# Six rounds of an output projection instead of four, and the small softmax-weight operations on GpSimd at ordinary priority

## The chip, the cores and the metric

The kernel runs on one core of a Trainium2 chip. The metric is the device time of one execution in microseconds; less is better. The engines are named as the profile names them: PE (matrix multiply; PEld is its weight load), DVE (vector), ACT (scalar and activation functions), POOL (GpSimd) and SP (issues the DMAs). Each engine works through its own instruction list in order.

## The reference, cut to what matters

One layer of an encoder, 1024 rows of 1024 columns, all in float32:

```
hn  = rms_norm(x);  q,k,v,glu,qm = split(hn @ w_in)
# A: 8 heads of 64, three dilated windows, merged by softmax weights of their denominators
attn = sum_p softmax_p(lse_p) * attention_p(rotary(norm(q)), rotary(norm(k)), v)
# B: gated unit, depthwise convolution over 31 rows, layer norm, silu
c    = silu(layer_norm(conv31(ga * sigmoid(gg))))
# C: 4 heads of 64 into 256 memory tokens
mo   = softmax(norm(qm) @ km.T / 8) @ vm
h    = x + concat(attn, c, mo) @ w_out          # 1024 -> 1024: eight blocks of 128 inputs
out  = h + (silu(fg) * fu) @ w_down,  fg,fu = split(conv3(rms_norm(h) @ w_up))   # 2816 wide
```

## The kernel before, in words

**Stages.** By time of the profiled execution: the input projection with the convolution and heads 0 to 5 beside it (to about 445 us), then heads 6 and 7 and the four memory heads, with the output projection reaching to 613 us, then the feed-forward part up to the end (1327.6 us).

**How the order is written.** Work is written as Python generators, advanced one step each tick (`Steps.tick`). Their order of emission, shifted by an offset from `PRIOS` (a larger number means that the instructions are wanted earlier), gives each instruction a priority; a scheduler with a model of times then fixes, before the run, each engine's list. At run time an instruction whose input is late holds up all behind it on its engine.

**The output projection** (`out_projections`, L1087). The concat of the three groups is eight blocks k of 128 inputs: k = 0 to 3 are the pairs of attention heads, 4 and 5 the convolution, 6 and 7 the pairs of memory heads. Each block and each half of its weights is split into a high and a low part, and a product takes three matmuls (high by high, high by low, low by high). `ROUNDS` lists which blocks are summed in one go: a round waits until its blocks are there, goes over the eight row tiles and two column halves (16 PSUM tiles, 3 matmuls of 512 columns per block in each, L1098), and `add_out` (L1110, DVE) adds each PSUM tile onto the residual `x_sb`. Two PSUM tiles (`proj`) are in use at a time. The last round also starts, row tile by row tile, the norm of the feed-forward part (L1163), and once its blocks are written the memory of the attention stage is released.

**Where blocks and weights wait.** The blocks of the last round lie in the tiles `mx_last`, the others in `mx` or `mx_more`, two blocks in each; `room_for` picks. The weights of `w_out` are loaded in the order of `ROUNDS` (L600 to L605), four blocks resident at a time (8 `w_hi`, 8 `w_lo`), and a block's weights are freed when its round is done.

**Softmax weights** (`softmax_weights`, L295), once per head, after its scores: the negated maxima and the denominators of the dilated pattern go through DRAM (8 stores, 4 loads, SP) to come into row order (`stat`); nine small DVE operations of 8 columns (L314 to L325) and one Exp on ACT (L318) make two weights per row; PE turns them (L329), DVE copies them (L332), SP stores them (L335, L336). `weigh` (L455) loads them spread over the head's columns (L467), multiplies and adds on POOL (L479, L484; DVE for the last half of pair 3), and ACT and DVE split the result into the block's parts (L291, L293). `head` also reloads q, k (L345 to L348) and v (L392, L393) on SP, converts q on POOL (L352 to L355), evacuates transposed probabilities on ACT and DVE (L272, L273) and adds halves of its output on POOL (L418).

Of the kernel before, what the change touches and what calls it, by code (L numbers as in the profile page):

```python
# [12 lines left out]
AF = mybir.ActivationFunctionType  # L13
OP = mybir.AluOpType
# [21 lines left out]

EARLY = 12

PRIOS = {"softmax_weights": 1000, "weigh": 500, "memory_values": -60, "memory_heads": 60, "add_out": 200}

ROUNDS = [[0], [4, 5], [1, 6, 7], [2, 3]]


def constants():
# [28 lines left out]
class Steps:  # L73
# [47 lines left out]
    def tick(self):  # L121
# [4 lines left out]
        for w in self.work[:]:  # L126
            with self.tc.high_priority(offset=PRIOS.get(w.__name__, 0)):
                if next(w, self) is self:
# [4 lines left out]
def block(tc, a, out):  # L133
    nc = tc.nc
    pe, act, dve, pool, sp = nc.tensor, nc.scalar, nc.vector, nc.gpsimd, nc.sync
# [23 lines left out]
    expo = cpool.tile([128, 4], F, name="expo")  # L159
# [20 lines left out]
    def count(key):  # L180
        stored[key] = stored.get(key, 0) + 1
# [23 lines left out]
    def room_for(k):  # L205


        if not keeping:
            return "mx_part"
        if k in ROUNDS[-1]:  # L210
            return "mx_last"
        before = [j for ks in ROUNDS[: round_of[k]] for j in ks if j not in kind_of]
        for name in keeping:
# [3 lines left out]

    round_of = {k: n for n, ks in enumerate(ROUNDS) for k in ks}

# [75 lines left out]
    def softmax_weights(h, stat, stat2):  # L295


        for k in range(8):
            sp.dma_start(st_d[h][k].rearrange("(r s) c n -> s r (c n)", r=4),
                         stat2[16 * k : 16 * k + 16].rearrange("s r c n -> s r (c n)"))  # L300
        yield
        there = stat[:, 1].rearrange("p u c n -> p u (c n)")
        sp.dma_start(there[0:64], st_d[h][1:8:2].rearrange("k p c n -> p k (c n)"))
        sp.dma_start(there[64:128, 0:3], st_d[h][2:7:2].rearrange("k p c n -> p k (c n)"))
        for c in range(2):
            sp.dma_start(stat[64:128, 1, 3, c], st_d[h][0, :, 1 - c])
        st.free("stat2")
        for _ in range(4):
            yield
        w = yield from st.new("w", [128, 2, 2, 4])  # L310
        wd = yield from st.new("wd", [128, 4, 2, 4])
        nm, d = (stat[:, :, :, :, i].rearrange("p g u c -> p g c u") for i in range(2))
        one = wd[:, 2]
        dve.tensor_tensor(one, nm[:, 0], nm[:, 1], OP.min)  # L314
        for g in range(2):
            dve.tensor_tensor(w[:, g], one, nm[:, g], OP.subtract)
        yield
        act.activation(w, w, AF.Exp)  # L318
        yield
        for g in range(2):  # L320
            dve.tensor_tensor(wd[:, g], w[:, g], d[:, g], OP.mult)
        dve.tensor_tensor(one, wd[:, 0], wd[:, 1], OP.add)
        dve.reciprocal(wd[:, 3], one)
        for g in range(2):
            dve.tensor_tensor(w[:, g], w[:, g], wd[:, 3], OP.mult)  # L325
        st.free("stat", "wd")
        yield
        ps = yield from st.new("z", [128, 512])
        pe.transpose(ps[0:16, 0:128], w.rearrange("p g c u -> p (g c u)"), ident)  # L329
        yield  # L330
        rows = yield from st.new("rows", [16, 128])
        dve.tensor_copy(rows, ps[0:16, 0:128])  # L332
        st.free("z", "w", "rows")
        for g in range(2):
            sp.dma_start(w_d[h][0, g, 64 : S + 64].rearrange("(u p) -> u p", p=128), rows[8 * g : 8 * g + 8])  # L335
            sp.dma_start(w_d[h][:, g, 0:64], rows[8 * g + 7 : 8 * g + 8, 64:128])  # L336
        count(("w", h))

    def head(h):
# [44 lines left out]
        else:  # L384
            st.kept["qk"] = 0
        st.start(softmax_weights(h, stat, stat2))
        while stored.get(("v", h // 4), 0) < NT:
            yield
# [171 lines left out]
    with tc.tile_pool(name="p1", bufs=1, side="right") as p1:  # L560
# [20 lines left out]
        def load_chunks(chunks):  # L581
            for c in chunks:
                w = 256 // c.n
                for k2 in range(KT // 2):
# [13 lines left out]
                    yield  # L598
            for k in sum(ROUNDS, []):
                for half in range(2):  # L600
# [486 lines left out]
        def out_projections():  # L1087
            for ks in ROUNDS:
                if ks is ROUNDS[-1]:
                    count("last round")  # L1090
                for k in ks:
                    while k not in mixed or (k, 1) not in wo:
                        yield
                for t in range(NT):
                    for half in range(2):
                        ps = yield from st.new("proj", [128, 512])
                        for n, (k, i, j) in enumerate(passes(ks)):
                            pe.matmul(ps, mixed[k][i][:, 128 * t : 128 * t + 128], wo[k, half][j],  # L1098
                                      start=(n == 0), stop=(n == 3 * len(ks) - 1))
                            if n % 6 == 5 and n < 3 * len(ks) - 1:  # L1100
                                yield
                        st.start(add_out(ps, x_sb[t][:, 512 * half : 512 * half + 512]))
                        yield
                    if ks is ROUNDS[-1]:
                        st.start(ffn["norm"](t))
                for k in ks:
                    st.free("w_hi", "w_lo", "w_hi", "w_lo", kind_of[k], kind_of[k])
# [258 lines left out]
```

## Time and profile before

| | us |
|---|---|
| median of 3 runs (lowest, highest) | 1325.08 (1323.47, 1330.56) |
| the profiled execution's own time | 1329.41 |
| its span on the core | 1327.6 |

Busy over the span: PE 1202.5 us (91%), DVE 857.2 us (65%), POOL 745.5 us (56%), ACT 629.1 us (47%). Times below are counted from the start of the span. A row of the timeline gives start, length, engine, line, operation and, in brackets, how long the engine had been idle before it and what it then waited for; a row of a group gives busy time and the mean ns of one instruction.

### The profile page before, as it was taken

How to read it: one execution, taken by the hardware profiler on the slowest of the kernel's cores; microseconds unless marked ns; L12 is line 12 of the kernel's file. 1: busy time of each engine (PE TensorE's matmuls, PEld its weight loads, DVE VectorE, ACT ScalarE, POOL GpSimd, SP SyncE). 2: the span in 40 equal slices, each digit the busy share in tenths (PEclk: the TensorE clock that was granted, in tenths of full speed). 3: DMA queues.
4: the chain of work that ended last, by engine and by line, in shares of the span. 5: the costliest groups of instructions: out<-in, count | busy, mean ns of one | idle time of the engine just before them, and what ended most of it. 6: DMA issues, size and time to landing. Idle time of an engine off the chain costs nothing. (4 is left out here: it accounts for less than half of the span.)

```text
span 1327.6 us, 18490 instructions
## 1 busy us (share of the span) xinstructions
PE 1202.5 (91%) x6287; PEld 1015.5 (76%) x6287; DVE 857.2 (65%) x1312; ACT 629.1 (47%) x1288; POOL 745.5 (56%) x721
## 2 busy tenths in 40 slices
PE   4899888799988587888798999999999999999997
PEld 4888887799967565676586888888888888888886
DVE  6748779786776555648668878888888652224222
ACT  5663165467865576425344444444444443333331
POOL 4834284595772443236557666666766645555552
PEclk8999988899979888899699999999999999999999
DMA  7363425565485641043122222222222254447443
GB/s 257 103 175 104 146 78 165 161 200 152 118 286 157 163 121 42 8 142 113 31 64 79 80 80 87 87 67 86 87 79 72 80 176 149 149 145 249 163 144 119
DMA packets 166554, 164.80 MB, mean 124 GB/s; under 512 B 20322, under 2 KB 125756, under 8 KB 166460
## 3 DMA queue, kind: packets, MB, share of 16 engines
q1 hardware_dynamic: 166460, 163.63, 40.0%
q8 instruction: 49, 0.80, 0.3%
q14 instruction: 45, 0.37, 0.1%
HBM read 121.51 MB, written 42.08 MB: 123 GB/s over the span
## 5 line engine op out<-in xcount | busy, mean ns | idle before, releaser
L916 PE MATMUL proj<-w_hi,hnT 128*128 128x256 f32 x896 | 191.7, 301 | 24.7 <-ACT raw L831 10.9
L1207 POOL TENSOR_TENSOR up_lo<-dn_raw,up_hi 128x512 fp32r<-128x512 f32 x88 | 131.5, 1516 | 118.4 <-ACT up_hi L1206 107.4
L916 PEld LDWEIGHTS proj<-w_hi,hnT 128*128 128x128 f32 x896 | 153.5, 203 | 28.3 <-ACT raw L831 11.7
L1207 POOL TENSOR_TENSOR up_lo<-up_sum,up_hi 128x512 fp32r<-128x512 f32 x88 | 153.2, 1751 | 26.8 <-ACT up_hi L1206 23.4
L1207 POOL TENSOR_TENSOR up_lo<-up_raw,up_hi 128x512 fp32r<-128x512 f32 x66 | 100.8, 1529 | 102.3 <-ACT up_hi L1206 94.7
L1207 DVE TENSOR_TENSOR up_lo<-dn_raw,up_hi 128x512 fp32r<-128x512 f32 x44 | 57.4, 1305 | 151.7 <-ACT up_hi L1206 144.1
L1206 ACT ACTIVATE up_hi<-dn_raw 128x512 fp32r<-128x512 f32 x132 | 75.2, 624 | 164.7 <-issue 115.0
L1333 PE MATMUL ps_dn<-up_lo,up_hi 128*128 128x512 f32 x352 | 137.0, 390 | 0.1
L1333 PE MATMUL ps_dn<-up_hi,up_lo 128*128 128x512 f32 x352 | 136.5, 389 | 0.0
L1333 PE MATMUL ps_dn<-up_hi 128*128 128x512 f32 x352 | 134.9, 389 | 0.0
L916 PE MATMUL proj<-w_lo,hnT 128*128 128x256 f32 x448 | 133.8, 299 | 0.6 <-POOL w_lo L623 0.6
L635 POOL TENSOR_TENSOR w_lo<-w_raw,w_hi 128x512 fp32r<-128x512 f32 x44 | 64.9, 1484 | 95.3 <-ACT w_hi L633 91.4
L1225 PE MATMUL ps_a<-A,up_hi 128*128 128x512 f32 x352 | 113.9, 395 | 0.0
L1225 PE MATMUL ps_c<-S,up_hi 128*128 128x512 f32 x352 | 110.7, 395 | 0.0
L418 POOL TENSOR_TENSOR u<-u,other 64x512 f32<-64x512 f32 (+2 forms) x40 | 44.5, 1121 | 88.6 <-ACT u L414 87.4
L916 PEld LDWEIGHTS proj<-w_lo,hnT 128*128 128x128 f32 x448 | 90.9, 203 | 1.2 <-POOL w_lo L623 1.2
L979 DVE SCALAR_TENSOR_TENSOR conv<-conv,cwT 128x1009 f32<-128x1009 f32 (+14 forms) x60 | 88.2, 1470 | 0.6
L1206 ACT ACTIVATE up_hi<-up_sum 128x512 fp32r<-128x512 f32 x88 | 54.6, 624 | 58.3 <-PE ps_c L1225 45.3
L278 PE MATMUL turn<-identr,prob 128*128 128x128 f32 x320 | 61.4, 299 | 21.3 <-DVE pt L273 14.6
L1225 PEld LDWEIGHTS ps_c<-S,up_hi 128*128 128x128 f32 x352 | 65.9, 187 | 16.1
L1225 PEld LDWEIGHTS ps_a<-A,up_hi 128*128 128x128 f32 x352 | 65.9, 187 | 16.0
L1333 PEld LDWEIGHTS ps_dn<-up_lo,up_hi 128*128 128x128 f32 x352 | 66.1, 188 | 14.5 <-POOL up_lo L1207 1.0
(234 smaller groups left out, 3127.1 us busy)
## 6 DMA issues: line engine op xcount, KB each, us to landing
up_raw<-w_up SPq DMA_DIRECT2D x92, 256.0 KB
dn_raw<-w_down SPq DMA_DIRECT2D x88, 256.0 KB
g_d<-yg SPq DMA_DIRECT2D x22, 512.0 KB
dn_raw<-g_d SPq DMA_DIRECT2D x44, 256.0 KB
x<-x SPq DMA_DIRECT2D x16, 512.0 KB
qk_d<-out SPq DMA_DIRECT2D x32, 256.0 KB
qk<-qk_d SPq DMA_DIRECT2D x16, 512.0 KB
w_raw<-w_in SPq DMA_DIRECT2D x40, 128.0 KB
```

What stands on the lines that cost most here:

```text
L278: pe.transpose(ps[:, i], blocks[g + i], ident)
L418: pool.tensor_tensor(o, o, m, OP.add)
L635: (dve if next(chunk_no) < EARLY else pool).tensor_tensor(lo, raw, f32(hi), OP.subtract)
L916: pe.matmul(ps[:, :256], lhs[i][:, k], c.parts[k][j], start=(k == 0 and i == 0 and j == 0), stop=(k == KT - 1 and i == 1))
L979: dve.scalar_tensor_tensor(acc[:, c0:c1], conv_in[i][:, c0 + k - 15 : c1 + k - 15], w, acc[:, c0:c1], OP.mult, OP.add)
L1206: act.activation(hi, src, AF.Copy)
L1207: adder.tensor_tensor(lo, src, f32(hi), OP.subtract)
L1225: pe.matmul(ps, w[i][:, k], ops[x][j][:, k], start=(first and n == 0), stop=(n == 3 * KH - 1), skip_group_check=not first)
L1333: pe.matmul(ps, gk[i][:, 128 * t : 128 * t + 128], wk[half][j], start=(k == 0 and m == 0), stop=(k == NF - 1 and m == 2))
```

## The change

The rounds are cut and put in another order; the weights of `w_out` and the places of the blocks follow from the same list (blocks 3 and 7, not 2 and 3, are now those of the last round). The raised priorities of `softmax_weights` and `weigh` are gone. The nine DVE operations of a head become nine POOL operations, in another form: the difference of the two maxima (twice, one for each sign), Relu and then Exp with scale -1 on ACT, and the reciprocal as the square of a power of -0.5 (`expo` holds -0.5).

```diff
-PRIOS = {"softmax_weights": 1000, "weigh": 500, "memory_values": -60, "memory_heads": 60, "add_out": 200}
+PRIOS = {"memory_values": -60, "memory_heads": 60, "add_out": 200}
-ROUNDS = [[0], [4, 5], [1, 6, 7], [2, 3]]
+ROUNDS = [[0], [4, 5], [1], [2], [6], [3, 7]]
@@ softmax_weights
-        dve.tensor_tensor(one, nm[:, 0], nm[:, 1], OP.min)
         for g in range(2):
-            dve.tensor_tensor(w[:, g], one, nm[:, g], OP.subtract)
+            pool.tensor_tensor(w[:, g], nm[:, g], nm[:, 1 - g], OP.subtract)
         yield
-        act.activation(w, w, AF.Exp)
+        act.activation(w, w, AF.Relu)
+        act.activation(w, w, AF.Exp, scale=-1.0)
         yield
         for g in range(2):
-            dve.tensor_tensor(wd[:, g], w[:, g], d[:, g], OP.mult)
-        dve.tensor_tensor(one, wd[:, 0], wd[:, 1], OP.add)
-        dve.reciprocal(wd[:, 3], one)
+            pool.tensor_tensor(wd[:, g], w[:, g], d[:, g], OP.mult)
+        pool.tensor_tensor(one, wd[:, 0], wd[:, 1], OP.add)
+        pool.tensor_tensor(wd[:, 3], one, expo[:, 0:1, None].to_broadcast([128, 2, 4]), OP.pow)
+        pool.tensor_tensor(wd[:, 3], wd[:, 3], wd[:, 3], OP.mult)
         for g in range(2):
-            dve.tensor_tensor(w[:, g], w[:, g], wd[:, 3], OP.mult)
+            pool.tensor_tensor(w[:, g], w[:, g], wd[:, 3], OP.mult)
```

## Rows read from the trace of the kernel before

**Rows 1.** Windows: from:to and length, busy time of each engine, PE clock, DMA.

```profile
449.00:461.00 12.00, 0.00 (x0) 0.00 (x0) 4.57 (x17) 5.38 (x16) 4.79 (x5) 0.61 0.38 91
449.00:545.00 96.00, 61.56 (x321) 48.30 (x321) 54.82 (x176) 64.17 (x171) 40.02 (x54) 0.80 0.30 83
545.00:578.00 33.00, 32.89 (x140) 26.28 (x139) 14.50 (x21) 4.66 (x7) 2.08 (x2) 0.97 0.00 0
760.00:800.00 40.00, 40.00 (x173) 32.14 (x172) 33.11 (x28) 18.01 (x27) 27.49 (x18) 1.00 0.27 90
```

**Rows 2.** Windows of the output projection's matmuls (L1098) alone: PE, PEld, clock, DMA.

```profile
449.00:545.00 96.00, 1.98 (x7) 1.16 (x7) 0.80 0.30 83
545.00:578.00 33.00, 31.48 (x130) 24.72 (x131) 0.97 0.00 0
```

**Rows 3.** Timeline of PE around the wait of round [1, 6, 7].

```profile
447.51 0.39 PE L1098 MATMUL proj<-w_hi,mx_more 128*128 128x512 f32 x1
...
461.60 1.94 PE L278 MATMUL turn<-identr,prob 128*128 128x128 f32 x8 [12.75 <-DVE pt L273]
...
464.67 2.26 PE L287 MATMUL o<-pt,v 128*128 128x256 f32 x9 [1.13 <-DMA v<-vr_d]
...
578.45 0.39 PE L1098 MATMUL proj<-w_hi,mx_last 128*128 128x512 f32 x1
```

**Rows 4.** Timeline of DVE: last step of blocks 2, 6 (both halves), 3 and 7.

```profile
462.66 1.10 DVE L293 TENSOR_TENSOR mx_last<-u,mx_last 128x512 fp32r<-128x512 f32 x1 [0.62 <-ACT mx_last L291]
...
501.16 1.09 DVE L293 TENSOR_TENSOR mx<-pairs_m,mx 128x512 fp32r<-128x512 f32 x1 [0.81 <-ACT w L318]
...
536.83 1.10 DVE L293 TENSOR_TENSOR mx<-pairs_m,mx 128x512 fp32r<-128x512 f32 x1
...
543.53 1.13 DVE L293 TENSOR_TENSOR mx_last<-u,mx_last 128x512 fp32r<-128x512 f32 x1 [0.22 <-ACT mx_last L291]
...
556.45 1.08 DVE L293 TENSOR_TENSOR mx<-pairs_m,mx 128x512 fp32r<-128x512 f32 x1
```

**Rows 5.** Timeline of DVE in round [1, 6, 7], one add per PSUM tile.

```profile
562.07 0.69 DVE L1110 TENSOR_TENSOR x<-proj,x 128x512 f32<-128x512 f32 x1 [1.38 <-PE proj L1098]
564.14 0.69 DVE L1110 TENSOR_TENSOR x<-proj,x 128x512 f32<-128x512 f32 x1 [1.38 <-PE proj L1098]
```

**Rows 6.** Timelines of ACT and SP in the gap of Rows 3.

```profile
451.73 1.10 ACT L291 ACTIVATE mx_last<-u 128x512 fp32r<-128x512 f32 x1 [0.18 <-POOL u L484]
457.82 0.21 ACT L318 ACTIVATE w<-w 128x16 f32<-128x16 f32 x1 [4.99 <-DVE w L316]
...
460.13 1.09 ACT L272 ACTIVATE pt<-turn 128x512 fp32r<-128x512 f32 x2
...
454.99 0.60 SPq L303 DMA_DIRECT2D stat<-st_d  x1
...
457.87 0.58 SPq L393 DMA_DIRECT2D v<-vr_d  x1
```

**Rows 7.** Groups by shape: small operations on DVE, then on POOL, whole span.

```profile
L316 DVE TENSOR_TENSOR w<-wd,stat 128x8 f32<-128x8 f32 x16 | 2.4, 189 | 0.2
...
L855 POOL TENSOR_TENSOR raw<-t,t 128x32 f32<-128x32 f32 x32 | 8.3, 258 | 4.4 <-ACT sq L832 2.0 <-POOL t L853 1.1
...
L165 POOL TENSOR_TENSOR r<-r,expo 128x4 f32<-128x4 f32 x42 | 47.1, 1124 | 1.8
L165 POOL TENSOR_TENSOR rv<-rv,expo 128x1 f32<-128x1 f32 x8 | 4.6, 581 | 0.3
```

**Rows 8.** Timelines: weights of head 7 ready (DVE), its output ready (POOL).

```profile
510.11 0.27 DVE L332 COPY rows<-z 16x128 f32<-16x128 f32 x1
...
527.49 1.42 POOL L418 TENSOR_TENSOR u<-u,other 64x448 f32<-64x448 f32 x2 [5.08 <-ACT u L414]
```

**Rows 9.** Line L314, whole span: durations min/median/max, idle time before it (us, times).

```profile
L314 DVE TENSOR_TENSOR wd<-stat x8: 152/165/288, 107.2 to 499.9; 128x8 f32<-128x8 f32 x8
...
  DMA stat<-st_d: 3.4, 1
```

## The prediction

> **What bounds the kernel now.** I read the page's share of busy time first, then windows of equal length over the span, then the windows of the stages around the change, then the timelines of PE, DVE, ACT and SP where PE has holes. In the feed-forward part PE is busy for 40.00 of 40 us at full clock, and the reader should see that nothing before it can shorten it: it only starts earlier or later [rows 1]. So the change is worth what it does to the time at which the last round begins, 578.45 us [rows 3]; what follows (norm, first feed-forward columns) hangs on that round and moves with it.
>
> Before it PE has a hole. From 449 to 545 us it is busy 61.56 of 96 us, at a mean granted clock of 0.80 (a mixture of its two levels, 2.4 and 1.2 GHz), and of this only 1.98 us is output projection; from 545 to 578 us it is full, and 31.48 of the 32.89 us are output projection [rows 1, 2]. The reason stands in the timelines. Round [1, 6, 7] filled its two PSUM tiles with block 1 alone by 447.51 us, and then waited for blocks 6 and 7, the memory heads [rows 3]. These become complete at 537.9 and 557.5 us; block 2 was complete at 463.8 us and waited for the last round, and block 3 at 544.7 us [rows 4]. PE thus holds back 31.5 us of a round until the memory heads are nearly done, while two thirds of the last two rounds' inputs are older.
>
> The worst piece of the hole is 12.75 us long, up to 461.60 us [rows 3]: no PE work at all. There ACT ended a split at 452.83 us and next in its list had the Exp of the softmax weights, which waited for DVE, which waited 3.4 us for the `stat` loads; the evacuation of finished transposes (`pt`) stood behind it and came at 460.13 us [rows 6, 9]. The weights' raised priority had put them first.
>
> **The change part by part.**
>
> *Rounds.* A row tile with three blocks takes 564.14 - 562.07 = 2.07 us [rows 5], 0.23 us per matmul, so a block costs 16 x 3 x 0.23 = 11.0 us. Blocks 1 and 2 leave the stretch behind the memory heads: 22.1 us less there. Block 6 alone stays (11.0 us), and half of it, the first four row tiles, may run before 545 us, since the first half of block 6 was split at 502.2 us and the second at 537.9 us [rows 4]. I take 22.1 us for this part, and call the half of block 6 a reserve against what follows.
>
> *The price of more rounds.* Four rounds have 64 adds on DVE, six have 96: 32 more of 0.69 us, 22 us [rows 5]. With the 32 matmul groups of rounds [1] and [2], PE would stand at 61.6 + 22.1 = 83.7 of the 96 us, DVE, with these rounds' 32 adds, at 54.8 + 22 - 3 (the small operations of heads 6 and 7) = 74 [rows 1, 7]. Both fit, but the stretch is a chain through PE, DVE and ACT, and each group and add can stand before a link of it. Lower bound: nothing, if all fall into idle time. Upper bound: each of the 32 adds delays the chain by its whole length, 22 us. I take 8: the 16 adds of round [1] are ready at the start, in the hole, and of the other 16, 11 us long, about three quarters (DVE's share when 74 of 96 us are busy) meet work that is wanted.
>
> *Priority.* With the weights at ordinary priority I expect `pt` to be ahead of them on ACT, at 452.8 instead of 460.1 us: 7.3 us. What is next late is v of head 6, issued at 457.87 us behind the `stat` loads (454.99 us) and needed for the gather at 464.67 us [rows 3, 6]; the loads of v and of head 7's q and k stand behind the same loads on SP, so they move forward too if the weights' DMAs lose their place. Bounds: 0, if the scheduler leaves the order or something else is late, and 12.75 us, the whole hole. I take 7.
>
> *The move to POOL.* Per head nine DVE operations go, 1.6 us at 0.17 to 0.19 us each [rows 7, 9]. On POOL eight of 0.26 us come (the nearest shape, 32 columns, is an upper guess for 8), and one power: 0.58 us at 1 column and 1.12 us at 4, so by the slope about 1.85 us at 8, and 1.1 us if it does not grow [rows 7]. That is 3.2 to 4.0 us, plus a Relu of 0.2 us on ACT: the path of a head's weights grows by 1.8 to 2.6 us. It is covered: head 7's weights are turned at 510.1 us and its output is complete on POOL at 528.9 us [rows 8], 18.8 us of slack less the loads. If that cover were gone, block 3 would be late by the excess alone, and it has 12.8 us to block 7 [rows 4]. POOL has room, 40.0 of 96 us busy [rows 1]. I price this part at 0. Behind a weight operation that waits for its load now stand POOL's adds of head outputs, the conversion of the next q and the weight splits; that is the price in the third rival.
>
> The Trainium skill, "GPSIMD Engine Reference", section "Engine selection", speaks against this part: element-wise work belongs on VectorE, GpSimd being about twice as slow with two inputs. The trace agrees in direction, 258 ns for 32 columns against 189 ns for 8 [rows 7]. By the rule the nine operations would cost 3.2 us for 1.6, which the same cover hides, so it says nothing against the sum, only for the second rival.
>
> *Sum.* -22.1 + 8 - 7 - 0 = -21, and 1 us of the reserve of block 6 (of 5.5): -22. The profiled execution took 1329.41 us (its span 1327.6 and 1.8 around it), so it would take 1307.4; it lay 4.3 us above the median of the runs, 1325.08, so as a median I predict 1303.
>
> **Rivals.**
>
> *The adds take it back.* DVE or the chain through it becomes the bound of the stretch: all 22 us of adds are paid, the rounds bring nothing, and only the 7 us of priority stay, 1318; without these, 1325. For it: ACT and DVE are busy for 64.2 and 54.8 of the 96 us and `add_out` has a raised priority of 200, ahead of the heads' own work. Against it: 41 us of DVE's stretch are idle [rows 1]. Chance 0.17.
>
> *Late weights.* At ordinary priority, over four engines and two DMA trips, head 7's weights come so late that block 3 is the last. It decides from a delay of 18.8 + 12.8 = 31.6 us on; a delay of 40 us leaves 1303 + 8 = 1311. For it: each of the chain's hand-overs now queues. Against it: the slack. Chance 0.08.
>
> *POOL as the blocked queue (slower).* The wait for `stat` doesn't vanish with the priority but moves to POOL, where the conversion of q, the sums of head outputs and the splits of the projection's weights stand behind it. One block of the kind seen, 7.3 us [rows 6], at each of the eight heads, is 58 us of held queue; it decides against the change when more than three of the eight (22 us) reach PE. With five, 36 us, less 22 of gain: 1339. For it: POOL's list is in order as DVE's is. Against it: only one of eight such waits held DVE before, for 3.4 us [rows 9]. Chance 0.12.
>
> *It runs better.* With rounds [1] and [2] in the hole, PE's clock stays up, the links on PE shorten too, and all 5.5 us of block 6 and the whole 12.75 us are won: -22.1 - 12.75 - 5.5 + 3 (adds) = -37, 1288. Before, the clock fell to a mean of 0.61 in the idle 12 us and stayed at 0.97 where PE was full [rows 1]. Chance 0.10.
>
> That the rounds do not move, because block 2 or its weights find no place, I hold for unlikely and count with the first rival: the buffers of block 0 are free long before 449 us, and four blocks of weights fit.
>
> **How the numbers follow.** Forecast 0.53 (1294 to 1314), the rivals 0.17, 0.08, 0.12 and 0.10 as above. Below 1288 and above 1326 I leave 0.05 and 0.13, so the range is 1288 to 1326. About 0.5%, 6.6 us, is what a measurement here can tell from no change. Faster by more: the forecast, late weights and the better case, 0.71, and half of the first rival, 0.08: 0.79. Within: the other half, 0.09. Slower: 0.12.
>
> **What would show it.** Right: matmuls of L1098 in every ten microseconds from 449 to about 490 us, no idle stretch of PE near 10 us there, the last round starting between 550 and 562 us, the feed-forward rows shifted but unchanged. The price of the adds: block 7's last split, 557.5 us before. Wrong: block 3 complete after block 7 (late weights); waits of POOL's weight operations for `stat`, and PE waiting for q, `w_lo` or the scores before 445 us (blocked POOL); the last round at 570 us or later with DVE full ahead of it (adds).

## The result, and the profile after

The changed kernel takes 1309.83 us, the median of 4 runs (1308.41 to 1312.53), beside 1327.82 us for the kernel before on the same chip (4 runs, 1323.47 to 1330.70): a ratio of 0.987, with a 95% interval of 0.9832 to 0.9907. Forecast were 1303, with a range of 1288 to 1326. The profiled execution took 1310.28 us (span 1308.5), 19.1 us less than that of before. Two numbers stand behind the 19.1, and neither is the one forecast: the last round begins 29.8 us earlier, and 10.7 us of that are given back after it.

First, windows of the changed kernel, with the columns of [rows 1]; the third reaches from 449 us to the start of the last round.

```profile
449.00:461.00 12.00, 8.90 (x43) 7.89 (x44) 6.75 (x11) 3.83 (x7) 2.75 (x4) 0.72 1.06 287
449.00:545.00 96.00, 81.18 (x432) 65.18 (x433) 72.96 (x190) 62.78 (x166) 44.05 (x70) 0.88 0.30 82
449.00:548.62 99.62, 84.34 (x443) 66.90 (x444) 76.46 (x196) 63.37 (x167) 44.05 (x70) 0.88 0.28 79
760.00:800.00 40.00, 39.51 (x167) 30.69 (x166) 32.36 (x26) 17.51 (x26) 27.12 (x17) 1.00 0.24 75
```

PE works in the hole where it did nothing before. From 449 to 545 us it is busy for 81.18 us instead of 61.56, and DVE for 72.96 instead of 54.82 (forecast: 83.7 and 74). But in the last window, far behind the change, PE is no longer full: 39.51 of 40 us, where it had 40.00.

The output projection's matmuls alone (L1099 is now their line), with the columns of [rows 2]: 33.85 us of them lie ahead of 545 us, where 1.98 us lay before.

```profile
449.00:545.00 96.00, 33.85 (x113) 20.31 (x114) 0.88 0.30 82
545.00:548.62 3.62, 2.29 (x10) 1.24 (x9) 1.00 0.00 0
```

The timeline of PE, for [rows 3], and that of DVE, for [rows 4]. The hole of 12.75 us has shrunk to one of 2.85, and the last round starts at 548.62 us instead of 578.45.

```profile
453.07 1.41 PE L287 MATMUL o<-pt,v 128*128 128x256 f32 x5 [2.85 <-DMA v<-vr_d]
...
548.62 0.39 PE L1099 MATMUL proj<-w_hi,mx_last 128*128 128x512 f32 x1
```

```profile
450.91 1.06 DVE L293 TENSOR_TENSOR mx<-u,mx 128x512 fp32r<-128x512 f32 x1
...
534.42 1.07 DVE L293 TENSOR_TENSOR mx<-pairs_m,mx 128x512 fp32r<-128x512 f32 x1
...
540.14 1.12 DVE L293 TENSOR_TENSOR mx_last<-u,mx_last 128x512 fp32r<-128x512 f32 x1
...
550.36 1.08 DVE L293 TENSOR_TENSOR mx_last<-pairs_m,mx_last 128x512 fp32r<-128x512 f32 x1 [0.47 <-ACT mx_last L291]
```

These are the last splits of blocks 2, 6, 3 and 7. Block 7 is complete at 551.4 us, only 6 us earlier than before, and block 3 still comes ahead of it, at 541.3. The blocks did not come much sooner; what changed is that nothing was left to catch up when they came.

The small operations on GpSimd, groups by shape: count, busy time and mean ns of one, then the idle time ahead.

```profile
L323 POOL TENSOR_TENSOR wd<-wd,expo 128x8 f32<-128x8 f32 x8 | 14.2, 1777 | 0.4
L321 POOL TENSOR_TENSOR wd<-w,stat 128x8 f32<-128x8 f32 x16 | 4.4, 295 | 4.6 <-ACT w L318 4.6
L322 POOL TENSOR_TENSOR wd<-wd 128x8 f32<-128x8 f32 x8 | 3.5, 433 | 0.4
L326 POOL TENSOR_TENSOR w<-w,wd 128x8 f32<-128x8 f32 x16 | 3.4, 235 | 0.4
L315 POOL TENSOR_TENSOR w<-stat 128x8 f32<-128x8 f32 x16 | 3.4, 227 | 7.1 <-DVE hl L866 6.4 <-DVE stat L239 0.6
L324 POOL TENSOR_TENSOR wd<-wd 128x8 f32<-128x8 f32 x8 | 2.8, 346 | 0.3
```

Together 31.7 us for eight heads, 4.0 us a head, the upper end of the 3.2 to 4.0 of the forecast; the power takes 1.78 us (estimated: 1.85).

**Where the 10.7 us go back.** In the feed-forward part the pairs of columns run in a steady loop of seven products of twelve matmuls. In the kernel before, a matmul of `ps_a` comes at 864.54 and the same one of the next pair at 884.14 us: 19.60 us, without a wait.

```profile
864.54 0.39 PE L1225 MATMUL ps_a<-A,up_hi 128*128 128x512 f32 x1
...
884.14 0.39 PE L1225 MATMUL ps_a<-A,up_hi 128*128 128x512 f32 x1
```

In the changed kernel (at about the same time, but further on in its pairs) it is this:

```profile
864.57 0.63 PE L1226 MATMUL ps_a<-A,up_hi 128*128 128x512 f32 x2
...
875.53 0.40 PE L1226 MATMUL ps_a<-A,up_lo 128*128 128x512 f32 x1
876.17 0.74 PE L1226 MATMUL ps_c<-S,up_hi 128*128 128x512 f32 x2 [0.24 <-ACT p L1278]
...
878.85 0.39 PE L1226 MATMUL ps_c<-S,up_lo 128*128 128x512 f32 x1
879.18 0.74 PE L1226 MATMUL ps_d<-A,up_hi 128*128 128x512 f32 x2
...
884.89 0.63 PE L1226 MATMUL ps_a<-A,up_hi 128*128 128x512 f32 x2
```

A pair takes 20.32 us. Matmuls start every 0.23 us, so the `ps_c` row could have come at 875.77 and comes 0.40 late; the `ps_d` row loses 0.10 in the same way; each of the two takes 0.11 longer as well, 0.74 instead of 0.63. That is the whole 0.72. The order of the products has changed: the scheduler, which makes each engine's list ahead of the run, now puts the last product of a pair (A22) and the S3 of the next back to back, and S4 (`ps_c`) close behind a copy on ACT (L1278). ACT's timeline shows what that copy stands behind:

```profile
874.06 1.06 ACT L1296 ACTIVATE yg<-yg 128x1024 f32<-128x1024 f32 x1 [2.33 <-DVE yg L1295]
875.02 0.62 ACT L1207 ACTIVATE up_hi<-up_sum 128x512 fp32r<-128x512 f32 x1
875.54 0.58 ACT L1278 ACTIVATE p<-ps_c 128x512 f32<-128x512 f32 x1
```

In the kernel before, the copy ended at 875.31 us, and S4 began 3.0 us after it, at 878.31:

```profile
874.73 0.58 ACT L1277 ACTIVATE p<-ps_c 128x512 f32<-128x512 f32 x1
```

No line of the diff lies there. The wait stands 16 times between 620 and 1080 us; 16 x 0.72 = 11.5 us, about the 10.7.

### The profile page after: what moved, and what is told of

Its sections match the earlier page's. It is cut to its first block, busy times and chain, and to the rows that moved or that the text cites. A ratio compares the mean times of both kernels' runs of the same rounds, so it can differ in the third digit from the quotient of the medians.

```text
span 1308.5 us, 18556 instructions
## 1 busy us (share of the span) xinstructions
PE 1197.1 (91%) x6287; PEld 1000.3 (76%) x6287; DVE 868.7 (66%) x1272; ACT 626.6 (48%) x1296; POOL 788.5 (60%) x793
## 4 chain that ended last, share of the span: by engine, by line
PE 46%; DVE 18%; issue 8%; ACT 7%; POOL 6%; DMA 5%; SPq 1%; POOLq 0%; ACTq 0%; DVEq 0%
PE ps_dn L1334 18%; PE ps_c L1226 6%; PE ps_d L1226 6%; PE proj L1099 4%; PE proj L917 3%; DVE yg L1295 3%; DVE conv L980 2%; DVE yu L1295 2%; PE o L287 2%; DMA v<-vr_d 2%; POOL up_lo L1208 2%; PE turn L278 2%; PE ps_a L1226 2%; ACT yu L1293 2%; DVE yg L1294 1%
## 5 line engine op out<-in xcount | busy, mean ns | idle before, releaser
L917 PE MATMUL proj<-w_hi,hnT 128*128 128x256 f32 x896 | 188.1, 298 | 23.7 <-ACT raw L832 12.9
L1208 POOL TENSOR_TENSOR up_lo<-up_raw,up_hi 128x512 fp32r<-128x512 f32 x66 | 116.0, 1760 | 68.8 <-PE ps_a L1226 46.3
L1226 PE MATMUL ps_c<-S,up_hi 128*128 128x512 f32 x352 | 113.5, 404 | 6.6 <-ACT p L1278 6.6
L1226 PE MATMUL ps_a<-A,up_hi 128*128 128x512 f32 x352 | 111.1, 396 | 0.0
L1221 DVE TENSOR_TENSOR up_sum<-up_raw,up_sum 128x512 f32<-128x512 f32 x40 | 59.0, 1476 | 50.4 <-POOL up_lo L1208 50.4
L1111 DVE TENSOR_TENSOR x<-proj,x 128x512 f32<-128x512 f32 x96 | 64.1, 682 | 25.0 <-PE proj L1099 24.9
L1293 ACT ACTIVATE yu<-cu,fwT 128x1024 f32<-128x1024 f32 x22 | 27.4, 1244 | 108.0 <-DVE cu L1286 106.3
```

The source lines that it names most:

```text
L917: pe.matmul(ps[:, :256], lhs[i][:, k], c.parts[k][j], start=(k == 0 and i == 0 and j == 0), stop=(k == KT - 1 and i == 1))
L1111: dve.tensor_tensor(dst, ps, dst, OP.add)
L1208: adder.tensor_tensor(lo, src, f32(hi), OP.subtract)
L1221: adder.tensor_tensor(t, x, y, OP.subtract)
L1226: pe.matmul(ps, w[i][:, k], ops[x][j][:, k], start=(first and n == 0), stop=(n == 3 * KH - 1), skip_group_check=not first)
L1293: act.activation(y, c, AF.Identity, scale=tap[1], bias=b)
```

## The experiments

Theory, after the comparison: the rounds did it ahead of the last round, by giving PE work in its idle stretches, and the order of the feed-forward pairs took a third of it back. Rivals: the priorities did it; or the 10.7 us were lost to contention of VectorE and GpSimd. Of the eight combinations of the three parts, seven were run (priorities with GpSimd were not): four have the old order of pairs (before, e2, e3, e4) and three the new one (the changed kernel, e1, e12).

In the ledger, "last round" is the start of its first matmul in the profiled execution; busy and idle are PE's from 449 us to there.

| | ratio to before (95%) | last round | busy | idle | clock | pairs |
|---|---|---|---|---|---|---|
| before | 1 | 578.45 | 94.90 | 34.55 | 0.84 | old |
| changed kernel | 0.9870 (0.9832 to 0.9907) | 548.62 | 84.34 | 15.28 | 0.88 | new |
| e1 rounds | 0.9868 (0.9841 to 0.9895) | 557.92 | 90.25 | 18.67 | 0.92 | new |
| e2 priorities | 0.9957 (0.9938 to 0.9976) | 578.14 | 100.72 | 28.42 | 0.81 | old |
| e3 GpSimd | 1.0008 (0.9991 to 1.0026) | 583.52 | 101.22 | 33.30 | 0.82 | old |
| e4 rounds, priorities | 0.9731 (0.9703 to 0.9758) | 547.36 | 86.89 | 11.47 | 0.95 | old |
| e5 changed, pairs of before | 0.9798 (0.9777 to 0.9819) | 552.10 | 88.67 | 14.43 | 0.88 | old |
| e6 before, pairs of after | 1.0077 (1.0054 to 1.0101) | 578.52 | 94.64 | 34.88 | 0.84 | new |
| e7 as e4, fewer adds | 0.9829 (0.9803 to 0.9856) | 548.92 | 85.80 | 14.12 | 0.91 | new |
| e8 as e2, idle rounds | 0.9970 (0.9952 to 0.9988) | 572.09 | 107.83 | 15.26 | 0.93 | old |
| e9 e5 with VectorE | 0.9701 (0.9681 to 0.9721) | 542.86 | 82.36 | 11.50 | 0.95 | old |
| e10 e4, weights first | 0.9747 (0.9733 to 0.9762) | 547.99 | 85.45 | 13.54 | 0.91 | old |
| e11 e4, `weigh` first | 0.9826 (0.9793 to 0.9858) | 553.37 | 87.39 | 16.98 | 0.92 | new |
| e12 rounds, GpSimd | 0.9851 (0.9829 to 0.9873) | 557.31 | 91.71 | 16.60 | 0.89 | new |

How far one profiled execution may be read: up to the last round e5 has the lists of the changed kernel, e9 those of e4, e6 those of before, and their starts differ by 3.5, 4.5 and 0.1 us. A difference of less than about 5 us in that column proves nothing; the ratios decide. The time from the last round to the end is clearer: in the eight profiled executions with the old order of pairs it is 746 to 752 us, in the six with the new one 756 to 762.

**e1 to e4: one part alone, and two together.** e1 keeps the old `PRIOS` and VectorE, e2 changes only `PRIOS`, e3 only the operations; e4 is:

```diff
-PRIOS = {"softmax_weights": 1000, "weigh": 500, "memory_values": -60, "memory_heads": 60, "add_out": 200}
+PRIOS = {"memory_values": -60, "memory_heads": 60, "add_out": 200}
-ROUNDS = [[0], [4, 5], [1, 6, 7], [2, 3]]
+ROUNDS = [[0], [4, 5], [1], [2], [6], [3, 7]]
```

> The new rounds alone; priorities and softmax-weight operations as before. Theory A (the rounds do it all): the last round starts within 3 us of 548.6, as with the whole change, and not at 578.5; the priorities are worth nothing. Theory B (the terms of the prediction): the rounds give 15 of the 29.8 us, so that the last round starts near 563, and the priorities give the rest. For the total: this program executes the feed-forward pairs in the second order (A22 and S3 of the next pair back to back, 20.32 us a pair against 19.60), as the changed kernel does. If that order costs about 10 us, A gives 1327.8 - 29.8 + 10 = 1308 and B 1323; if the order costs nothing, A gives 1298 and B 1313.

> The two raised priorities taken away alone; rounds and operations as before, feed-forward pairs in the order of before. By the prediction's term the 12.75 us hole before 461.6 us shrinks by 7 us and the last round starts near 571, total 1321. Theory A: the hole shrinks but block 7 is complete at about the same time, the last round starts within 2 us of 578.5, total 1326 to 1330.

> The softmax-weight operations on GpSimd alone; rounds and raised priorities as before, feed-forward pairs in the order of before. By the prediction the move costs nothing: last round within 2 us of 578.5, total 1326 to 1330. The rival of a blocked GpSimd queue: the last round is 5 us later or more, total above 1333.

> Rounds and priorities of the change, the small operations left on VectorE. This program executes the feed-forward pairs in the order of before. Theory F (the order of the pairs costs the changed kernel about 10 us): the last round starts near 549 and the total is 1309.8 - 10 = 1300, below the changed kernel. Rival G (the 10 us are lost whatever the order, to contention between VectorE and GpSimd after the last round): total 1307 to 1312. Rival H (the move to GpSimd is needed for the gain ahead of the last round): the last round starts at 556 or later.

The rounds alone move the last round by 20.5 us, between theories A and B: more than the terms of the prediction, less than the whole. The priorities alone leave it where it was in the profiled execution (which lies 3.5 us above e2's median); the runs say 5.7 us less, 3 to 8. GpSimd alone makes no difference in the runs (its last round starts 5.1 us later, about what single executions differ by). A blocked queue is visible all the same. The line of the first GpSimd operation in e3, its idle time by what ended it (us, times):

```profile
its engine sat idle before it (us, times) until:
  DMA stat<-st_d: 17.5, 2
  DVE stat L239: 6.5, 2
```

And e4, two thirds of the change, is faster than all of it: 1295.9 us, with the old order of pairs. That agrees with theory F, but GpSimd is missing there as well, so e5 and e6 change the order alone.

**e5 and e6: the order of the pairs, in each kernel.** One group of matmuls of one pair gets a lower priority, which is enough to tip the order of those that follow.

```diff
 # e5, on the changed kernel
-        product(pd, "S3", w3, True)
+        with tc.high_priority(offset=-20 if ct == 3 else 0):
+            product(pd, "S3", w3, True)
 # e6, on the kernel before
-        product(pd, "A22", w4, False)
+        with tc.high_priority(offset=-60 if ct == 2 else 0):
+            product(pd, "A22", w4, False)
```

> The changed kernel with one group of matmuls (S3 of the fourth feed-forward pair) at a priority lower by 20, all else the same. Up to the third pair every engine's list is that of the changed kernel; from the fifth pair on the pairs run in the order of before. Theory F (the order of the pairs costs 0.72 us a pair): the last round starts at 548.6 as in the changed kernel, a pair takes 19.6 us, and with 14 to 17 pairs in that order 10 to 12 us are saved, less about 2 for the disturbed fourth pair: total 1298 to 1302. Rival G (contention between VectorE and GpSimd after the last round): a pair stays near 20.3 us or the time is lost elsewhere, total 1308 to 1311.

> The kernel before with one group of matmuls (A22 of the third feed-forward pair) at a priority lower by 60, all else the same; from the fourth pair on the pairs run in the order of the changed kernel. Theory F: a pair takes 20.3 us, the last round starts at 578.5 as before, total 10 to 13 us above before, 1338 to 1343 where before has 1328 to 1331. Rival G: within 3 us of before.

Theory F holds in both directions: the order takes 0.77% from the kernel before (10 us, 7 to 13), and putting it back gives the changed kernel 0.72% (10 us, 4 to 15). A pair takes 19.60 us in e5 (857.77 to 877.37) and 20.34 in e6 (854.67 to 875.01). PE's waits between 800 and 1000 us (sum, times, longest): none in e5; the changed kernel and e6 have one group each, the same one.

```profile
PE ps_c L1226 <- ACT p L1278: 2.5, 10, 0.3
```

```profile
PE ps_c L1225 <- ACT p L1277: 3.0, 10, 0.6
```

**e7: sixteen adds fewer.** Blocks 1 and 2 share a round again, the rest as e4.

```diff
-ROUNDS = [[0], [4, 5], [1], [2], [6], [3, 7]]
+ROUNDS = [[0], [4, 5], [1, 2], [6], [3, 7]]
```

> Rounds [0], [4, 5], [1, 2], [6], [3, 7], the rest as in e4 (priorities gone, small operations on VectorE): 16 adds of 0.69 us fewer, 11 us of VectorE, and the same blocks out of the stretch behind the memory heads. Theory A (adds are paid, by the prediction's rate 0.25 us for each of the 32): the last round starts 4 us before the 547.4 of e4, near 543. Theory C (the adds of these rounds hide, and what counts is that TensorE has matmuls to do): it starts at 547 or later, since the round cannot begin before block 2 is complete at 451.8. This program runs the feed-forward pairs in the order of the changed kernel, so the total is by theory F about 10 us above the one that the last round alone would give: 1302 by A, 1306 or more by C.

The last round starts at 548.92 us, but 1.6 us beside e4 are less than one execution can tell. The ratio, less the 0.77% of the order of pairs, is 0.975 beside e4's 0.973: 3 us slower, from 3 faster to 9 slower. Taking away 16 adds gained nothing that can be seen, and theory A's 4 us lie just outside. A loss from the later start, behind block 2, may hide a small gain.

**e8: matmuls that nobody needs.** As e2, with blocks 1 and 2 multiplied once more ahead of round [1, 6, 7], each result left unread in PSUM.

```diff
 # out_projections, ahead of the third round
+    for t in range(NT):
+        for half in range(2):
+            ps = yield from st.new("proj", [128, 512])
+            ... the 3 matmuls of the block
+            st.free("proj")
```

> As e2 (priorities gone, rounds of before), and besides the matmuls of blocks 1 and 2 are done once more ahead of round [1, 6, 7], 96 of 512 columns, 22 us of TensorE, whose results nobody reads. Theory K (the clock): e2 had 28.4 us without TensorE work from 449 us to the last round, but a granted clock of 0.81, and gained nothing; work that fills the idle stretches keeps the clock up, so although TensorE has 22 us more to do, the last round starts no later than in e2, 570 to 580, at a clock of 0.9 or more. Rival W (TensorE's clock is of no account, the added work falls in the way of the chain): it starts 5 to 22 us later than in e2, 583 to 600, with a total of 1330 to 1347.

Windows of e2, then of e8, from 449 us to the last round and from 500 to 520 us:

```profile
449.00:578.14 129.14, 100.72 (x466) 80.07 (x467) 69.14 (x195) 67.30 (x176) 41.29 (x54) 0.81 0.22 61
500.00:520.00 20.00, 14.56 (x62) 11.71 (x61) 6.74 (x24) 11.12 (x28) 7.68 (x12) 0.59 0.07 27
```

```profile
449.00:572.09 123.09, 107.83 (x561) 88.01 (x560) 66.35 (x189) 65.90 (x170) 39.43 (x53) 0.93 0.23 62
500.00:520.00 20.00, 14.01 (x79) 11.73 (x78) 8.52 (x27) 12.36 (x30) 8.71 (x12) 0.85 0.09 27
```

With 96 matmuls more, 22 us, the last round starts no later, and by the runs the kernel is as fast as e2 (0.9970 beside 0.9957, with overlapping intervals). The idle time shrank by 13.2 us, and busy time rose by only 7.1. In the second window, behind the last of the added matmuls (494.4 us), 14 us of busy time hold 79 matmuls instead of 62: the mean granted clock of the stretch is 0.85 instead of 0.59 of its upper level, 2.4 GHz. The mix of shapes is not the reason. From 494.9 us to the last round both kernels run the same 64 transposes, which take 379 ns each in e2 and 321 in e8, and the same 28 matmuls with v, in e2 and then in e8:

```profile
L287 PE MATMUL o<-pt,v 128*128 128x256 f32 x28 | 10.8, 474 | 8.2 <-ACT pt L272 5.3 <-DMA v<-vr_d 2.8
```

```profile
L287 PE MATMUL o<-pt,v 128*128 128x256 f32 x28 | 7.9, 374 | 5.9 <-ACT pt L272 5.6 <-DVE pt L273 0.3
```

Theory K holds here: with the idle stretches filled, the granted clock stayed higher. e2 fits it: its hole was closed (5.86 us of work between 450 and 460, none before) and its idle time fell by 6.1 us, but its busy time grew by 5.8 us, of which six matmuls more (466 instead of 460) are only 1.4, at a clock of 0.81 instead of 0.84.

**e9: GpSimd or the disturbed pair?** e5, the softmax weights back on VectorE.

> e5 with the small operations on VectorE instead of GpSimd: rounds and priorities of the change, S3 of the fourth feed-forward pair lower by 20, pairs in the order of before. It has e4's work ahead of the last round and e5's disturbed fourth pair. Theory P (the move to GpSimd costs what lies between e4 at 1295.9 and e5 at 1303.5): as e4, 1294 to 1299, the last round within 2 us of 547.4. Rival N (the disturbed fourth pair costs it): as e5, 1301 to 1305.

1293.34 us, the lowest median of all. The nudge costs nothing that the runs show (0.9701 beside e4's 0.9731, with overlapping intervals), so what lies between e9 and e5 is the move to GpSimd: 0.97% of 1330, 13 us (9 to 17); between e4 and e5 it is 9 (4 to 14). PE's matmuls of heads 6 and 7 with v (L287), from 449 to 542 us, in e9 and then in the changed kernel:

```profile
L287 PE MATMUL o<-pt,v 128*128 128x256 f32 x55 | 12.6, 320 | 2.0 <-ACT pt L272 1.7 <-DMA v<-vr_d 0.2
```

```profile
L287 PE MATMUL o<-pt,v 128*128 128x256 f32 x56 | 14.7, 359 | 7.3 <-DMA v<-vr_d 3.5 <-ACT pt L272 3.3 <-DVE pt L273 0.3
```

5 us more of waits stand there, 3.5 of them for the load of v (0.2 in e9, 0.3 in e4). That goes with the cost and does not prove it: e11, on VectorE, waits 2.0 us at the same place.

PE's time from 449 us to the last round does show where the cost lies. PE is idle for 15.28 and 14.43 us in the changed kernel and e5, for 11.47 and 11.50 in e4 and e9. It is busy for 84.34 us with 443 matmuls and 88.67 with 458 in the first two, for 86.89 with 476 and 82.36 with 459 in the others. For 459 matmuls in each, at 0.23 us for one more or fewer, that is about 88 and 89 us against 83 and 82 (an estimate), at a clock of 0.88 instead of 0.95. So some 3 us are more waiting and some 6 the same matmuls taking longer, 9 together. Which operations on GpSimd make the holes is not settled.

**e10 to e12: which priority, and GpSimd with the priorities.** e10 puts `"softmax_weights": 1000` back into e4's `PRIOS`, e11 `"weigh": 500`; e12 is the changed kernel with both.

> e4 with the raised priority of softmax_weights (1000) put back, that of weigh left out. In e1, with both priorities, the last round starts at 557.9, in e4, with neither, at 547.4. By the step of the prediction (the Exp of the weights waits on ScalarE for the loads of stat and holds the evacuation of transposes) this priority is the one that costs: last round 555 to 559, total 1303 to 1307. Rival: it is that of weigh; then 546 to 549 and 1294 to 1298.

> e4 with the raised priority of weigh (500) put back, that of softmax_weights left out. By the step of the prediction this costs nothing ahead of the last round: it starts within 3 us of 547.4. Rival: this priority is what costs in e1, the last round starts at 555 to 559. This program runs the feed-forward pairs in the order of the changed kernel, so the total is about 10 us above what the start alone gives: 1306 or 1315.

> Rounds of the change and small operations on GpSimd, with both raised priorities as before: the changed kernel less the removal of the priorities. If the priorities cost 10 us here as they do with the operations on VectorE (e1 against e4), the last round starts near 559, and the total is 1309.8 + 10 = 1320. If the wait for stat on GpSimd's queue, 24 us in e3, is a price of its own with these rounds, it starts at 563 or later, 1324 or more. If the move makes the priorities harmless, because ScalarE's Exp no longer waits, it starts near 549. The feed-forward pairs are in the order of the changed kernel.

e10 is not told apart from e4 (0.9747 and 0.9731, the intervals overlap), against the step of the prediction that named this priority. ACT shows that what the step describes does happen in e10, the Exp waiting and `pt` behind it:

```profile
453.91 0.21 ACT L318 ACTIVATE w<-w 128x16 f32<-128x16 f32 x1 [3.55 <-DVE w L316]
454.15 1.09 ACT L272 ACTIVATE pt<-turn 128x512 fp32r<-128x512 f32 x2
```

But PE, which had nothing to do at that place before, now has round [1]: from 449 to 461 us it is busy for 8.66 us, and from 449 to 500 us it waits for `pt` only once, for 1.2 us. e11 starts its last round 6 us later; less the 0.77% of its order of pairs its ratio would be 0.975, so it too is not told apart from e4. Together they do cost: e1, corrected in the same way, is 0.979, 8 us (2 to 14) above e4. Which does it stays open. On GpSimd the same removal gains nothing that the runs show (0.9851 with both, 0.9870 without), though its profiled last round is 8.7 us earlier.

## Why the prediction was right, and where its steps were not

**What bounds.** Right: the start of the last round is what the change moves, and the hole from 449 us is where it moves it.

**Rounds.** Direction and place were right: matmuls in the hole, the start near block 7's completion. The term of the adds was mis-sized: +8 us for 32 of them, where e1's 20.5 us (the clock's gain among them) leave 22.1 + 1 - 20.5 = 2.6, and e7 shows no gain from 16 fewer. The adds fell beside PE work that was now there; DVE's 72.96 us were foreseen, but charging their busy share to the chain was the mistake. The runs say so more firmly than one execution: e1, less the 0.77% of the order of pairs, is 28 us faster than the kernel before (23 to 33), where the terms for the rounds gave 15. Of the signs named, PE has output projection in every ten microseconds from 449 to 489 us and no idle stretch above 2.85 us there; the last round starts 1.4 us ahead of the "between 550 and 562 us". One reading was wrong, though nothing in the sum hangs on it: of the five blocks of the last two rounds not "two thirds" were older, but two (1 and 2); 6 and 3 were complete only at 537.9 and 544.7 us [rows 4].

**The clock.** The forecast counted idle time and left the clock to the fourth rival. Of the 29.8 us, 19.3 are less idle time (34.55 - 15.28) and 10.6 less busy time (94.90 - 84.34) of PE. About 4 of the 10.6 are not the clock's: the view of the kernel before has 460 matmuls there and that of the changed kernel 443, and the 17 missing ones, 0.23 us each, are output projection that now runs ahead of 449 us. The other 6.6 are the same work in less time, at a mean granted clock of 0.88 instead of 0.84. e8 shows this cause by itself: there the filled stretches shortened matmuls that came after them (474 to 374 ns). The rival's condition came true; its 1288 did not, for the two next points.

**Priorities.** -7 us was the size that both together have (5.7 alone, 8 with the new rounds, uncertain by 3 and by 6). In the change itself, with the weights on GpSimd, the runs show no gain from it (e12). The reason given, the Exp of the weights ahead of `pt`, is not borne out: e10 has that priority back, the Exp holds `pt` for 3.55 us again, and no loss can be seen, since round [1] gives PE work meanwhile. In part, then, this term and that of the rounds counted the same hole. Nor were the 7.3 us all the Exp's: between it and `pt` stood a split of `w_out` weights (459.47 us, L633) that waited 1.44 us for its own load.

**GpSimd at 0.** The price per head was right, 4.0 us; the price at the end was not: 0 when the move is the only change (e3), 9 to 13 us beside the other two (e4 and e9 against e5). The 0 was read from one cover: "head 7's weights are turned at 510.1 us and its output is complete on POOL at 528.9 us". That cover held. In the changed kernel the two stand at 507.8 and 526.1 us, 18.3 us apart instead of 18.8, and block 3 is complete 10 us ahead of block 7:

```profile
507.76 0.27 DVE L333 COPY rows<-z 16x128 f32<-16x128 f32 x1
```

```profile
524.69 1.42 POOL L419 TENSOR_TENSOR u<-u,other 64x448 f32<-64x448 f32 x2 [5.41 <-ACT u L415]
```

What failed is the step from this one path to the whole stretch: the loss is PE's waiting and clock from 449 us on (e9), which the sum had no term for. The blocked queue of the third rival was seen in e3, 17.5 us in two waits for `stat`, and cost nothing by the runs; in the changed kernel the same line (L315) shows no such wait. And the ratio of the two engines was read from unequal sizes, 32 columns against 8: on 8 columns the same multiplication (L321) takes 295 ns on GpSimd and took 184 on VectorE.

**What follows moves with it.** This step failed: "the feed-forward rows shifted but unchanged". They were re-ordered, for 10 us (e5, e6). The last row of [rows 1] did say that PE is full there; it did not say that the next program would have the same order.

So 1310 lies inside the range because three misjudged terms nearly cancel: a better last round (-29.8 for -22), which already holds GpSimd's price, with 10.7 given back behind it makes -19.1. That they cancel is luck; that the gain comes, and where, is not.

## What to carry to other kernels

Where an accumulation can start with any complete input, cut its rounds so that TensorE finds work in each idle stretch: here 22 us of matmuls in the holes cost nothing that the runs show, even when nobody read them (e8). Where a scheduler writes the lists, an edit can tip the order of a steady loop that it doesn't touch; compare that loop's period (19.60 and 20.32 us) before reading the total, or the loop's change is taken for the edit's. And a part that is free alone (e3) can cost 10 us in company, so the parts are worth timing in both settings: without GpSimd, and with the old order of pairs, this change is worth 2.7 to 3.0% (e4, e9) instead of 1.3%.

## What the runs showed of the hardware that was not expected

One add of 128x512 on VectorE, 0.67 us at 613.31 us, where GpSimd is idle, took 5.44 us in the changed kernel just behind the last round (L1184, 601.49 us), beside GpSimd operations that follow each other closely:

```profile
601.42 2.53 POOL L1208 TENSOR_TENSOR up_lo<-up_sum,up_hi 128x512 fp32r<-128x512 f32 x2
601.49 5.44 DVE L1184 TENSOR_TENSOR x<-x,x 128x512 f32<-128x512 f32 x1 [4.04 <-POOL x L1183]
...
603.90 1.27 POOL L1221 TENSOR_TENSOR up_sum<-up_raw,up_sum 128x512 f32<-128x512 f32 x1
605.12 1.27 POOL L1208 TENSOR_TENSOR up_lo<-up_sum,up_hi 128x512 fp32r<-128x512 f32 x1
```

In e9 the same operation, beside the same ones, took 1.75 us, and it was GpSimd that slowed down, from 1.27 to 1.7 us each:

```profile
595.94 2.95 POOL L1207 TENSOR_TENSOR up_lo<-up_sum,up_hi 128x512 fp32r<-128x512 f32 x2
596.01 1.75 DVE L1183 TENSOR_TENSOR x<-x,x 128x512 f32<-128x512 f32 x1 [4.05 <-POOL x L1182]
...
597.79 1.66 DVE L1184 TENSOR_TENSOR x<-x,x 128x512 f32<-128x512 f32 x1
...
598.86 1.71 POOL L1220 TENSOR_TENSOR up_sum<-up_raw,up_sum 128x512 f32<-128x512 f32 x1
```

The lists don't decide it: e4 and e9 have the same ones up to there, and show 5.43 and 1.75 us; the changed kernel and e5 likewise, 5.44 and 1.75. The Trainium skill, "SBUF — State Buffer", section "Who interferes with whom", has a VectorE operation with two SBUF inputs and a GpSimd operation that reads SBUF exclude each other for the length of an instruction, the one that comes first holding the port. The trace agrees that they exclude each other; but the wait covered four GpSimd operations in a row, 4.9 us, and not one. The difference, 3.7 us in one operation behind the last round, comes and goes between executions of the same lists, so it belongs to no part of this change.
